# Order of the compressed values' first projection against the keys' GELU in a two-layer decoder trunk

## The chip, the cores and the metric

The kernel runs on one core of a Trainium2 chip. Its time is the device time of one execution in microseconds (us), and the median of several runs is compared. One execution was also taken by the hardware profiler; all rows shown are from it. Engines: PE is TensorE's matmul, PEld its weight load, DVE VectorE, ACT ScalarE, POOL GpSimd, SP SyncE, which here only issues transfers. L714 is line 714 of the kernel.

## The reference

Two layers; each has an input projection into many columns, three token mixers (a convolution, a sparse attention "NSA", a latent attention "MLA"), a cross-attention and a SwiGLU. The change lies in the part of NSA that makes compressed keys and values, and in the projections around it:

```python
z = h @ w_in[layer]                      # 512 tokens, 1024 in
u_glu, q_nsa, kv_nsa, g_nsa, c_q, c_kv, k_rope, g_merge = jnp.split(z, split_at, axis=-1)

def compress_blocks(tok, pos, w1, b1, w2, n_cmp):        # once for keys, once for values
    idx = CMP_STRIDE * arange(n_cmp)[:, None] + arange(CMP_BLOCK)[None, :]   # 31 windows of 32 tokens
    blk = tok[:, idx] + pos[:, None, :]
    blk = ...reshape(bsz, n_cmp, GROUPS, CMP_BLOCK * HEAD_DIM)               # 2048 long
    return gelu(blk @ w1 + b1) @ w2                                          # 2048 -> 256 -> 64

lc = einsum('bqghd,bcgd->bghqc', qb, k_cmp) * scale + bias_c                 # compressed scores
pc = softmax(lc); o_cmp = einsum('bghqc,bcgd->bqghd', pc, v_cmp)
# beside it a selected and a window branch, with the same queries
```

## The kernel before, in words

All matmuls are in float32 made of parts: `unit` and `hilo` split a weight tile or an activation into a high part (ScalarE, L93 to L96) and a remainder (VectorE, L94, L97), and `mm3` (L86 to L88) multiplies three combinations of them. `hTh` and `hTl` hold the normed input so split, `wh` and `wl` (three buffers each) the weights. `fm_blocks` loads two column blocks of 128 (2 x 512 KB) into one of two buffers "raw" and splits them one after the other, each when a `wh` is free. `fm_steps` is one projection: eight steps of three matmuls over 512 tokens, 24 matmuls.

In a layer's `mix` two strands run together. The main strand is the attention: units of scores, softmax and mixture, first the four MLA heads, then the NSA branches. In the MLA part it turns probabilities by TensorE (L865), splits them (PTh by ScalarE, PTl by VectorE L94) and multiplies them with the values one turn later (L878 to L882), with the next head's scores (L843 to L847) between. The other strand is the generator `work`, the filler: `pump(n)` takes n steps of it between the main strand's turns (six in the MLA part). `braid(main, other)` takes two steps of the one and one of the other. So the order of the program is written out by hand, and each engine runs its instructions in an order fixed at compile time, in which what is written first goes first wherever it was expected to be ready. In `work`:

- `projected(windows, i)` projects the tokens of keys (i = 0) or values (i = 1), and `windows` gathers the 31 windows with the position term into `xf` (buffer "gB", four VectorE adds, L649) and splits them into `xt` (L93, L94). The values' `xt` takes the two buffers "BT", used by the keys' weights before and by the bias tables afterwards.
- `compress_in(i)` is the first product, `blk @ w1`: two loads of 1 MB into "raw", eight steps of a split (tile `w`) and four matmuls (L697, L698), into one bank "mm" of PSUM that is held until the GELU. PSUM has three banks "mm".
- `compress_out(i)` has three steps: the GELU (L705 to L710, tile `h`, also in buffer "gB"); its turn by two transposes L714, the split `hT` (L96, L97) and the load of the second weights; and the second product into `kc` or `vc`.
- `projected(stacked_keys, b)` and `projected(stacked_queries, h)` project keys and queries and stack their parts (L409, L410, L416 to L419).
- `conv_steps(m)` projects the two halves of one conv block (16 steps; the bank of the first half, `pa`, is held until both are there), then runs 31 taps on VectorE (L585, L587) at low priority.

`done` and `until` order the strands: the compressed scores (L998, bias added by L1005) ask for "group 0", the product with the compressed values (L1070) for "values". `begin` loads the bias tables (L984) into "BT", and later into "gB". Beside all this, GpSimd's queue issues loads for the SwiGLU of the same layer, one after every few products ("paced").

Of the kernel before, what the change touches and what calls it, by code (L numbers as in the profile page):

```python
# [22 lines left out]
KD = D // 128  # L23
# [10 lines left out]
Z_A, Z_B, Z_Q = 0, 512, 1024  # L34
Z_KC, Z_VC, Z_KS, Z_VS, Z_KW, Z_VW = 1536, 1664, 1792, 1920, 2048, 2176
# [17 lines left out]
def kernel(ctx, tc, x, mem, positions, rel_bias, norm_mix, norm_xattn, norm_mem, norm_ffn, norm_final,  # L53
# [20 lines left out]
    def new(tag, shape=(128, 512), dt=F32, name=None):  # L74
        return (odd if tag in ODD else sb).tile(list(shape), dt, name=name or tag, tag=tag, bufs=BUFS[tag])

    def bank(tag, name=None):
        return ps.tile([128, 512], F32, name=name or f"ps_{tag}", tag=tag, bufs=PBUFS[tag])
# [20 lines left out]
    def load(parts):  # L99
        raw = new("raw", (128, 2048))  # L100
        for view, src in parts(raw):
            nc.sync.dma_start(view, src)
        return raw

    def unit(src, shape):

        n = math.prod(shape)
        h = new("wh", (128, 1024), F32R)
        l = new("wl", (128, 1024), F32R)
        names = " ".join("abc"[:len(shape)])  # L110
        kw = dict(zip("abc", shape))
        hv = h[:, :n].rearrange(f"p ({names}) -> p {names}", **kw) if len(shape) > 1 else h[:, :n]
        lv = l[:, :n].rearrange(f"p ({names}) -> p {names}", **kw) if len(shape) > 1 else l[:, :n]
        hilo(hv, lv, src)
        return hv, lv

    def fm_blocks(w, cols, kt):

        per = 2048 // (kt * 128)
        for i in range(0, len(cols), per):  # L120
            c = cols[i:i + per]
            n = len(c)

            def parts(raw):
                rv = raw[:, :kt * n * 128].rearrange("p (k c) -> p k c", k=kt)
                j = 0
                while j < n:
                    e = j + 1
                    while e < n and c[e] == c[e - 1] + 128:
                        e += 1  # L130
                    yield (rv[:, :, j * 128:e * 128],
                           w[:, c[j]:c[j] + (e - j) * 128].rearrange("(k p) c -> p k c", p=128))
                    j = e
            raw = load(parts)
            rv = raw[:, :kt * n * 128].rearrange("p (k c) -> p k c", k=kt)
            for j in range(n):
                yield unit(rv[:, :, j * 128:(j + 1) * 128], (kt, 128))

    def fm_steps(o, wu, xs, kt, cols=((0, 512),)):
        wh, wl = wu  # L140
        for c0, c1 in cols:
            for k in range(kt):
                yield
                xh, xl = xs(k)
                mm3(o[:, c0:c1], wh[:, k, :], wl[:, k, :], xh[:, c0:c1], xl[:, c0:c1], k == 0, k == kt - 1)
# [325 lines left out]
    def mix(l, x_src, g_mix, x_now, more_x, spill_x, turns):  # L471
        W = w_in[l]
# [98 lines left out]
        def conv_steps(m):  # L571
            for i, wu in enumerate(fm_blocks(W, [Z_A + m * 128, Z_B + m * 128], KD)):
                p = bank("mm")
                yield from fm_steps(p, wu, hx, KD)
                if i == 0:
                    pa = p
            u = new("u", (128, T + TAPS - 1))
            nc.gpsimd.memset(u[:, 0:TAPS - 1], 0.0)
            th = new("ca", name="th")
            nc.scalar.activation(th, p, AF.Tanh, scale=0.5)  # L580
            nc.vector.scalar_tensor_tensor(u[:, TAPS - 1:], th, 1.0, pa, op0=OP.add, op1=OP.mult)
            c = us[m] = new("ca", name="ca")

            tc.cur_priority += 100000
            nc.vector.tensor_scalar(c, u[:, 0:T], cw[:, m, 0:1], cb[:, m:m + 1], op0=OP.mult, op1=OP.add)  # L585
            for j in range(1, TAPS):
                nc.vector.scalar_tensor_tensor(c, u[:, j:j + T], cw[:, m, j:j + 1], c, op0=OP.mult, op1=OP.add)  # L587
            tc.cur_priority -= 100000
# [33 lines left out]
        X = {}  # L622
        K2 = {}
        Q2 = [None] * HEADS
        blocks = fm_blocks(W, [Z_KC, Z_KS, Z_KW, Z_VC] + [Z_Q + 128 * i for i in range(4)], KD)

        def projected(then, *args):
            p = bank("mm")
            yield from fm_steps(p, next(blocks), hx, KD)
            then(p, *args)  # L630
# [42 lines left out]
        def compress_in(i):  # L673
            p = bank("mm")
            b1 = new("vec", (128, 256), name="b1")[0:64]
            vec = (cmp_b1_k, cmp_b1_v)[i]
            nc.scalar.dma_start(b1, bass.AP(tensor=vec.tensor, offset=vec[l].offset, ap=[[0, 64], [1, 256]]))
            hidden[i] = p, b1
            w1 = (cmp_w1_k, cmp_w1_v)[i][l]

            if i == 0:
                w = [t[:, j] for t in (new("BT", (128, 2, 512), F32R, name="w1") for _ in range(2)) for j in range(2)]
            else:
                t = new("o8", (128, 4, 512), F32R, name="w1")
                w = [t[:, j] for j in range(4)]
            w = [v.rearrange("p (k c) -> p k c", k=2) for v in w]
            for k in range(16):
                if k % 8 == 0:
                    raw = load(lambda raw: [(raw.rearrange("p (k c) -> p k c", k=8),
                                             w1[k * 128:(k + 8) * 128, :].rearrange("(k p) c -> p k c", p=128))])  # L690
                    rv = raw.rearrange("p (k c) -> p k c", k=8)
                if k % 2 == 0:
                    wh, wl = w[k % 4:k % 4 + 2]
                    hilo(wh, wl, rv[:, k % 8:k % 8 + 2, :])
                    yield
                x = X[i][k // 8][:, k % 8, :, :]
                nc.tensor.matmul(p[:, 0:256], x, wh[:, k % 2, :], start=k == 0, stop=False)  # L697
                nc.tensor.matmul(p[:, 0:256], x, wl[:, k % 2, :], start=False, stop=k == 15)  # L698
# [44 lines left out]
        done = set()  # L743
# [10 lines left out]
        def braid(main, other):  # L754

            while True:
                for _ in range(2):
                    if next(main, end) is end:
                        return
                    yield  # L760
                if next(other, end) is not end:
                    yield
# [350 lines left out]
        def work():  # L1113

            yield from projected(windows, 0)
            cmp_k, cmp_v = compress_in(0), compress_in(1)
            out_k, out_v = compress_out(0), compress_out(1)
            yield from conv_steps(1)
            yield from braid(projected(stacked_keys, 0), cmp_k)
            yield from braid(projected(stacked_keys, 1), cmp_k)  # L1120
            yield from cmp_k
            yield from projected(windows, 1)
            next(out_k)
            yield from projected(stacked_queries, 0)
            next(out_k)
            yield from braid(projected(stacked_queries, 2), cmp_v)
            next(out_k)
            yield from braid(projected(stacked_queries, 4), cmp_v)
            yield from cmp_v
            next(out_v)  # L1130
            done.add("group 0")
            yield from projected(stacked_queries, 6)
            next(out_v)
            third = conv_steps(2)
            yield from islice(third, 8)
            next(out_v)
            done.update(("values", "group 1"))
            yield from third
            yield from conv_steps(3)

            jobs = {84 + 3 * t: (conv_stats, t) for t in range(NT)} | {99 + 3 * m: (conv_swish, m) for m in range(4)}
            for n, _ in enumerate(chain(merge_steps(2, w_branch_mla[l], o_mla), merge_steps(0, w_branch_conv[l], cS))):
                if n in jobs:
                    yield
                    job, i = jobs[n]
                    job(i)
                yield
# [5 lines left out]
        kv_raw = load(lambda raw: [(raw.rearrange("p (k c) -> p k c", k=2),  # L1153
                                    w_ukv[l].rearrange("(k p) c -> p k c", p=128))])
        filler = work()
        means = bank(next(idle))
        for i, q in enumerate(sq):
# [263 lines left out]
    for l in range(L):  # L1421
# [55 lines left out]
        blocks = fm_blocks(w_xq[l], [128 * h for h in range(4)], KD)  # L1477
# [209 lines left out]
        W = w_gate_up[l]  # L1687
# [150 lines left out]
```

## Time and profile before

| | |
|---|---|
| median of 3 runs | 1897.95 us (1897.93 to 1900.44) |
| the profiled execution | 1898.13 us; span from first to last instruction 1896.4 us |
| granted TensorE clock | 0.999 of full speed |
| busy, share of the span | PE 99%, PEld 87%, DVE 80%, ACT 55%, POOL 14% |
| mixer stage with the change, layer 0 | about 95 to 215 us |
| the same, layer 1 | about 1030 to 1155 us |

A row of the timeline has start, duration, engine, line and operation, written tile and read tiles, the shape, a count, and in brackets how long the engine stood idle before it and for whom. A matmul's duration is modelled and overlaps the next; the distance of two starts is the better measure. A row of a tile has the line, engine and operation, the count, then the shortest, median and longest duration in ns, and the first and last start.

### The profile page before, as it was taken

To read this page: it belongs to the slowest core of one execution; us is meant where nothing else is said; L and a number is where in the kernel's file an instruction comes from. 1 tells how busy PE (TensorE), PEld (TensorE's weight loads), DVE (VectorE), ACT (ScalarE), POOL (GpSimd) and SP (SyncE) were. 2 spreads that over 40 slices of the span, in tenths; PEclk is the share of its full clock that TensorE was granted. 3 is DMA by queue.
4 is the path that set the end of the run, shared out by engine and by line. 5 is a ranking of instruction groups with operands and counts; after the bars stand their busy time and mean duration, and the time that the engine had idled before them with its cause. 6 is when DMAs were issued, how large, how long until landed. Compare 5 with 4: busy or idle time off the path is not lost.

```text
span 1896.4 us, 29494 instructions
## 1 busy us (share of the span) xinstructions
PE 1877.0 (99%) x10988; PEld 1643.5 (87%) x10988; DVE 1509.8 (80%) x2754; ACT 1045.7 (55%) x1952; POOL 269.6 (14%) x433
## 2 busy tenths in 40 slices
PE   9999999999999999999999999999999999999998
PEld 8887888888887999998888878888888879999986
DVE  7999898764466899998869999986645678999886
ACT  5366557763355645456543765676633465454564
POOL 1211111111122211100022111111112221110000
PEclk9999999999999999999999999999999999999999
DMA  6666554455866666656566665435566766766664
GB/s 188 164 155 185 143 129 127 123 147 157 238 180 161 187 163 186 185 181 197 180 181 164 163 197 129 127 100 136 157 182 177 216 165 159 202 164 163 209 191 159
DMA packets 217644, 318.52 MB, mean 168 GB/s; under 512 B 16352, under 2 KB 153843, under 8 KB 217500
## 3 DMA queue, kind: packets, MB, share of 16 engines
q1 hardware_dynamic: 183116, 216.39, 35.9%
q0 software_dynamic: 31872, 94.39, 23.9%
q10 hardware_dynamic: 2512, 5.85, 0.8%
q8 instruction: 86, 1.41, 0.3%
q14 instruction: 58, 0.48, 0.1%
HBM read 307.13 MB, written 97.54 MB: 213 GB/s over the span
## 4 chain that ended last, share of the span: by engine, by line
PE 87%; DVE 5%; issue 4%; ACT 2%; DMA 1%; POOL 1%; POOLq 0%; SPq 0%; DVEq 0%; ACTq 0%
PE ps_mm L86 14%; PE ps_mm L88 14%; PE ps_mm L87 14%; PE ps_s L86 3%; PE ps_s L88 3%; PE ps_s L87 3%; PE ps_t L86 2%; PE ps_t L87 2%; PE ps_t L88 2%; PE ps_t L1083 2%; PE ps_pv L86 1%; PE ps_pv L88 1%; PE ps_pv L87 1%; PE ps_mm L1374 1%; PE ps_mm L1373 1%
## 5 line engine op out<-in xcount | busy, mean ns | idle before, releaser
L93 ACT CAST wh<-raw 128x1024 fp32r<-128x1024 f32 (+3 forms) x419 | 422.8, 1012 | 498.0 <-PE ps_mm L87 123.5
L94 DVE TENSOR_TENSOR wl<-raw,wh 128x1024 fp32r<-128x1024 f32 (+3 forms) x419 | 488.6, 1172 | 221.6 <-ACT wh L93 218.4
L86 PE MATMUL ps_mm<-hTh,wh 128*128 128x512 f32 (+1 forms) x1152 | 414.6, 360 | 0.5 <-DVE kc L94 0.5
L87 PE MATMUL ps_mm<-hTl,wh 128*128 128x512 f32 (+1 forms) x1152 | 411.2, 357 | 0.0
L88 PE MATMUL ps_mm<-hTh,wl 128*128 128x512 f32 (+1 forms) x1152 | 410.5, 357 | 0.5 <-DVE wl L94 0.5
L88 PEld LDWEIGHTS ps_mm<-hTh,wl 128*128 128x128 f32 x1152 | 217.8, 189 | 32.7 <-DVE wl L94 1.3
L86 PEld LDWEIGHTS ps_mm<-hTh,wh 128*128 128x128 f32 x1152 | 217.9, 189 | 29.4 <-issue 1.3
L87 PEld LDWEIGHTS ps_mm<-hTl,wh 128*128 128x128 f32 x1152 | 217.9, 189 | 26.3 <-issue 0.7
L587 DVE SCALAR_TENSOR_TENSOR ca<-u,vT,ca 128x512 f32<-128x512 f32 x240 | 177.5, 747 | 2.9
L466 POOL DMA_DIRECT2D up<-in_w_gate_up_dram x128 | 85.0, 664 | 538.6 <-PE ps_mm L88 380.9
L466 POOL DMA_DIRECT2D down<-in_w_down_dram x132 | 85.3, 646 | 478.6 <-PE ps_mm L88 255.2
L93 ACT CAST PTh<-ps_t 128x512 fp32r<-128x512 f32 (+4 forms) x136 | 70.6, 519 | 53.2 <-PE ps_t L1083 39.6
L1046 ACT ACTIVATE P<-P,ss 128x512 f32<-128x512 f32 (+3 forms) x128 | 71.6, 560 | 49.2 <-DVE ss L1043 48.2
L86 PE MATMUL ps_s<-rh,wh 128*128 128x256 f32 x320 | 90.6, 283 | 0.0
L87 PE MATMUL ps_s<-rl,wh 128*128 128x256 f32 x320 | 90.6, 283 | 0.0
L88 PE MATMUL ps_s<-rh,wl 128*128 128x256 f32 x320 | 90.6, 283 | 0.0
L94 DVE TENSOR_TENSOR PTl<-ps_t,PTh 128x512 fp32r<-128x512 f32 (+2 forms) x120 | 71.6, 598 | 9.0 <-ACT PTh L93 7.9
L1054 ACT ACTIVATE P<-P,sr 128x512 f32<-128x512 f32 (+3 forms) x128 | 63.3, 555 | 16.9 <-DVE sr L1052 16.8
L86 PE MATMUL ps_mm<-op,wh 128*128 128x512 f32 (+1 forms) x192 | 68.8, 359 | 0.0
L88 PE MATMUL ps_mm<-op,wl 128*128 128x512 f32 (+1 forms) x192 | 68.4, 356 | 0.3
L87 PE MATMUL ps_mm<-op,wh 128*128 128x512 f32 (+1 forms) x192 | 68.0, 355 | 0.0
L86 PEld LDWEIGHTS ps_s<-rh,wh 128*128 128x128 f32 x320 | 61.4, 192 | 0.0
(567 smaller groups left out, 4652.0 us busy)
## 6 DMA issues: line engine op xcount, KB each, us to landing
up<-in_w_gate_up_dram POOLq DMA_DIRECT2D x128, 320.0 KB, 4.4
down<-in_w_down_dram POOLq DMA_DIRECT2D x132, 256.0 KB, 4.3
raw<-in_w_in_dram SPq DMA_DIRECT2D x32, 1024.0 KB
raw<-in_w_gate_up_dram SPq DMA_DIRECT2D x60, 512.0 KB
raw<-up SPq DMA_DIRECT2D x40, 512.0 KB
raw<-down SPq DMA_DIRECT2D x40, 512.0 KB
raw<-in_w_down_dram SPq DMA_DIRECT2D x30, 512.0 KB
raw<-in_w_in_dram SPq DMA_DIRECT2D x26, 512.0 KB
```

Source lines behind the costliest of these rows:

```text
L86: nc.tensor.matmul(o, lh, rh, start=start, stop=False)
L87: nc.tensor.matmul(o, lh, rl, start=False, stop=False)
L88: tick(nc.tensor.matmul(o, ll, rh, start=False, stop=stop))
L93: nc.scalar.copy(hi, src)
L94: nc.vector.tensor_tensor(lo, src, f(hi), op=OP.subtract)
L466: d = nc.gpsimd.dma_start(dst, src, accum_op=op) if op else nc.gpsimd.dma_start(dst, src)
L587: nc.vector.scalar_tensor_tensor(c, u[:, j:j + T], cw[:, m, j:j + 1], c, op0=OP.mult, op1=OP.add)
L1046: nc.scalar.activation(p[:, c], p[:, c], AF.Exp, bias=s[:, k:k + 1], scale=-1.0, accum_out=s[:, 4 + k:5 + k])
L1054: nc.scalar.activation(P[k], P[k], AF.Copy, scale=r[:, k:k + 1])
L1083: nc.tensor.transpose(tp[:, w:w + 128], P[k][:, j * 128:(j + 1) * 128], ident)
L1373: nc.tensor.matmul(accs[t], xh, u[0][:, k, :], start=j == 0, stop=False)
L1374: nc.tensor.matmul(accs[t], xh, u[1][:, k, :], start=False, stop=False)
```

## The change

The load pairs change, because blocks must come in the order of use: keys, selected keys, window keys, queries 0, values, queries 1, 2, 3 (each block of queries is two heads). In `work` the values' projection with its windows moves behind the step that turns the keys' GELU (second step of `compress_out(0)`). The values' first product is no longer braided with queries 1 and 2 but with queries 2 and with the first half of the third conv block (eight steps), which was behind queries 3 before. "group 0" is marked after queries 1.

```diff
-        blocks = fm_blocks(W, [Z_KC, Z_KS, Z_KW, Z_VC] + [Z_Q + 128 * i for i in range(4)], KD)
+        blocks = fm_blocks(W, [Z_KC, Z_KS, Z_KW, Z_Q, Z_VC] + [Z_Q + 128 * i for i in range(1, 4)], KD)
...
             yield from cmp_k
-            yield from projected(windows, 1)
             next(out_k)
             yield from projected(stacked_queries, 0)
             next(out_k)
-            yield from braid(projected(stacked_queries, 2), cmp_v)
+            yield from projected(windows, 1)
             next(out_k)
+            yield from projected(stacked_queries, 2)
+            done.add("group 0")
             yield from braid(projected(stacked_queries, 4), cmp_v)
+            third = conv_steps(2)
+            yield from braid(islice(third, 8), cmp_v)
             yield from cmp_v
             next(out_v)
-            done.add("group 0")
             yield from projected(stacked_queries, 6)
             next(out_v)
-            third = conv_steps(2)
             yield from islice(third, 8)
             next(out_v)
             done.update(("values", "group 1"))
             yield from third
```

## The prediction

> **What bounds the kernel now.** First the core's span with the granted clock, and the page's line of busy times: TensorE decides.
>
> ```profile
> core 0: 1896.4 us, clock 0.999
> ```
>
> ```profile
> PE 1877.0 (99%) x10988; PEld 1643.5 (87%) x10988; DVE 1509.8 (80%) x2754; ACT 1045.7 (55%) x1952; POOL 269.6 (14%) x433
> ```
>
> The change neither adds nor removes a matmul, so it can only act on the gaps between them. Second, then, the list of TensorE's waits, cut to the stretch of each layer where the change lies (first layer 0, then layer 1; columns: what waited, for whom, us in total, times, longest).
>
> ```profile
> PE ps_pv L881 <- DVE PTl L94: 1.2, 1, 1.2
> PE ps_mm L714 <- DVE h L710: 0.4, 1, 0.4
> PE ps_t L86 <- DVE op L410: 0.4, 1, 0.4
> PE ps_mm L698 <- DVE w L94: 0.3, 1, 0.3
> PE ps_mm L86 <- DVE kc L94: 0.3, 1, 0.3
> PE ps_pv L880 <- ACT PTh L93: 0.2, 1, 0.2
> ```
>
> ```profile
> PE ps_pv L881 <- DVE PTl L94: 1.2, 1, 1.2
> PE ps_mm L88 <- DVE wl L94: 0.5, 1, 0.5
> PE ps_mm L714 <- DVE h L710: 0.4, 1, 0.4
> PE ps_mm L86 <- DVE kc L94: 0.3, 1, 0.3
> PE ps_pv L880 <- ACT PTh L93: 0.2, 1, 0.2
> ```
>
> Both layers show the same cluster: L880, L881 and L714 wait one after the other, mostly for VectorE. Third, the timeline of TensorE gives its full price, since a stream that stopped also restarts slowly. The first two rows show the undisturbed distance of matmuls of 512 columns. From L847 on come L847, L880, L881 and L882, four of that width, and the two transposes L714, in layer 0 and then in layer 1.
>
> ```profile
> 158.04 0.39 PE L846 MATMUL ps_s<-op 128*128 128x512 f32 x1
> 158.26 0.39 PE L847 MATMUL ps_s<-op 128*128 128x512 f32 x1
> ...
> 161.69 0.33 PE L714 MATMUL ps_mm<-ident,h 62*128 62x62 f32 x2 [0.44 <-DVE h L710]
> 161.96 0.50 PE L86 MATMUL ps_mm<-hTh,wh 128*128 128x512 f32 x1
> ```
>
> ```profile
> 1096.72 0.39 PE L847 MATMUL ps_s<-op 128*128 128x512 f32 x1
> ...
> 1100.37 0.51 PE L86 MATMUL ps_mm<-hTh,wh 128*128 128x512 f32 x1
> ```
>
> The two rows are 0.22 apart; the times are rounded, and over longer runs it is 0.23. Undisturbed, then, this takes 4 x 0.23 and 0.27 for L714 (161.96 less 161.69), 1.19 us. It takes 3.70 and 3.65, so 2.51 and 2.46 us are lost, 4.97 us in all. Against the listed waits of a layer (1.2, 0.4 and 0.2, 1.8 us) that is a factor of 1.4, which I use for other waits below.
>
> Fourth, why VectorE is late: the 10 us that hold the cluster's main wait (columns: us, then busy us and count of PE, PEld, DVE, ACT, POOL, and the granted clock), and the rows of the tiles h (the GELU) and xf (the values' windows), with first and last start in layer 0.
>
> ```profile
> 151.00:161.00 10.00, 8.63 (x48) 6.87 (x46) 9.78 (x21) 6.90 (x16) 0.95 (x2) 1.00 0.49 133
> ```
>
> ```profile
> L714 PE MATMUL ps_mm<-ident,h x4: 221/246/270, 161.7 to 190.2; 62*128 62x62 f32 x4
> L705 DVE TENSOR_TENSOR h<-ps_mm,b x2: 410/414/417, 155.7 to 181.9; 62x256 f32<-62x256 f32 x2
> ...
> L710 DVE SCALAR_TENSOR_TENSOR h<-h x2: 406/412/418, 161.2 to 186.5; 62x256 f32<-62x256 f32 x2
> ```
>
> ```profile
> L649 DVE TENSOR_TENSOR xf<-ps_mm,vT x8: 659/672/677, 96.7 to 153.5; 64x496 f32<-64x496 f32 x8
> ```
>
> ```profile
> L94 DVE TENSOR_TENSOR xt<-xf,xt x8: 402/410/419, 99.5 to 155.0; 128x248 fp32r<-128x248 f32 x8
> ```
>
> In the code xf and the GELU's h1 share the one buffer "gB". The trace agrees: L705 starts at 155.7, when the last split xt that reads xf (155.0, 0.41 long) is over. So the keys' GELU stands behind the whole burst of the values' windows (4 x 0.67 and 4 x 0.41, 4.3 us of VectorE), and the softmax's split PTl stands between its five steps.
>
> **The change part by part.**
>
> **The order.** Now the turn of the GELU (L714) comes ahead of the values' projection. By then h1 has only the keys' old xf ahead of it, gone since about 100 us; the keys' product ends one projection and one turn of the attention ahead of the burst, whose four L649 end at 154.2: 154.2 less 4 x 0.67, 24 x 0.23 and some 1.5 is about 144 (an estimate), so L705 can start there and not at 155.7. Between it and L714 lies one projection, 24 matmuls of 0.23 us and a turn of the attention, as now lies between L705 of the values (181.9) and its L714 (190.2); of the two turns in layer 0 only one is in the list of waits, and the values' isn't. So I take the cluster's 4.97 us as gone. Bounds: 4.97 gone to nothing gone.
>
> **The burst by itself.** It stays, some 10 us after the GELU's start instead of ahead of it, and can make the next split late. The nearest rows are the keys' windows, which start at 96.7: their neighbourhood has the wait for op L410 (0.4) in layer 0 and for wl L94 (0.5) in layer 1, 0.9 us, times 1.4 makes 1.26 us. Bounds: 0, because none of the listed waits of layer 0 falls between 144 and 158, while the burst ran, and 4.97, the whole cluster again.
>
> **PSUM banks.** "mm" has three. Now the compressed keys' product holds one while the values' hidden sum holds another, hence the wait for kc: 0.3 in each layer, times 1.4 and twice 0.84 us, which goes, since the hidden sum begins only after it. In its place conv's first half (pa) is held over the last queries and the turn of the values' GELU. The second half must then wait for a bank from the turn (hT, read last by L97) or from the queries (op L410):
>
> ```profile
> L97 DVE SCALAR_TENSOR_TENSOR hT<-ps_mm,hT x1: 254/254/254, 193.9 to 193.9; 128x124 fp32r<-128x124 f32 x1
> ```
>
> ```profile
> L998 PE MATMUL ps_s<-kc,op x4: 276/277/277, 188.0 to 188.4; 128*128 128x64 f32 x4
> ```
>
> ```profile
> 189.26 0.40 PE L86 MATMUL ps_mm<-hTh,wh 128*128 128x512 f32 x1
> ```
>
> L97 ends at 194.15, 3.85 us after L714 (190.3); one turn of the attention (from the scores L998 to the next projection's matmul) covers 1.25 (189.26 less 188.0). So the bounds are 0 and 2.6 us a layer. The same kind of shortage cost 0.42 (kc). I take a quarter of the way from 0.42 to 2.6, 0.97, as the kc row is the only one that is such a wait: +1.93 us in both layers.
>
> **Loads.** The pairs of one load are now [keys' window, queries 0] and [values, queries 1]; the queries 0 and 1 were one transfer and become halves of two others, one more issue on SP's queue a layer (0.4 us, idle otherwise). The first projection's second half of weights is asked for when the first half is split, as now; its wait (w L94, 0.3) I leave. The load of conv's pair moves ahead of it on SP. ScalarE's load of b1 and GpSimd's four small memsets of xt move with their steps; both have 5 us and more until their readers, and behind the memsets in GpSimd's queue stand only the paced loads for the later down- and up-projection. Cost nothing, unless the third rival holds.
>
> **Values ready later.** vc comes one half of conv later: 24 x 0.23 and 1.25, 6.8 us.
>
> ```profile
> L738 DVE CAST vc<-vc x1: 282/282/282, 197.7 to 197.7; 32x256 fp32r<-32x256 f32 x1
> L1070 PEld LDWEIGHTS ps_pv<-PTh,vc x1: 187/187/187, 217.4 to 217.4; 128*128 128x128 f32 x1
> ```
>
> Its reader comes 19 us after it, so this costs nothing; without that cover it would be 6.8 us.
>
> **The bias table.** Its second half takes the buffer of the values' windows, free when the first projection ends. In the program that end moves from step 89 of the filler to step 97, and the compressed scores L998 are written after step 96; so in time it moves from 181.9 to about 188.0. (The mark "group 0", which they ask for, falls at step 73 and not 89: reached either way, so its own move costs and gains nothing.)
>
> ```profile
> L1005 DVE TENSOR_TENSOR Pc<-ps_s,BT x4: 223/235/253, 189.9 to 235.0; 128x62 f32<-128x62 f32 x2, 128x46 f32<-128x46 f32 x2
> L984 SPq DMA_DIRECT2D BT<-vd x2: 366/368/371, 172.0 to 181.9; - x2
> ```
>
> ```profile
> 195.33 0.43 DVE L94 TENSOR_TENSOR PTl<-ps_t,PTh 128x256 fp32r<-128x256 f32 x1
> ```
>
> ```profile
> 307.11 4.59 DMA BT<-vd
> ```
>
> ```profile
> 200.47 0.28 PE L881 MATMUL ps_pv<-PTl,op 128*128 128x256 f32 x1
> ```
>
> Asked for at 188.0 and 0.37 plus 4.59 us on its way, it lands near 193.0, and the second L1005 would run at 190.1: VectorE would stand still for 2.9 us, with all behind it. Its next split PTl (195.8 at its end) is read at 200.5, 4.7 us later, so 0 on TensorE; without that cover 2.9 us a layer. The Trainium skill's page "DMA: Bandwidth & Descriptors" (Anatomy of one DMA) gives 2.0 us plus bytes over 436 GB/s for GpSimd's queue, an estimate of 3.2 us for these 512 KB: by it VectorE would stand for 1.5 us. The trace's 4.59 for the same table decides.
>
> **Sum.** -4.97 - 0.84 + 1.26 + 1.93 = -2.62 us. The profiled execution took 1898.13 (span 1896.4 and 1.7 around it), 0.2 above the median of 1897.95; so 1895.5 against it and 1895.3 for the median.
>
> **The rivals.** *All waits go:* neither burst nor bank costs anything; -5.81, 1892.1 us. For it: no wait while the burst ran; against it: three banks are few, and VectorE is busy for 9.8 of 10 us here.
>
> *The wait only moves:* VectorE's work is the same and its queue full, so the late split comes back at the burst's new place, as large; 1897.9. For it that busy share; against it that the values' GELU, after an equal projection, made nobody wait.
>
> *The weights' load comes too late (slower):* there are two "raw" buffers, and between the two halves of the first projection's weights now stands conv's load, while [queries 2, queries 3] still holds the other. If queries 3 is split only after conv's first weights, the second half waits for two loads in a row.
>
> ```profile
> 167.95 5.84 DMA raw<-in_cmp_w_v_dram
> ```
>
> ```profile
> 144.65 0.39 ACT L93 CAST wh<-raw 128x256 fp32r<-128x256 f32 x1
> ```
>
> Two loads of 5.84 and five splits of about 1 to 1.2 come to some 17 us; cover are the 6.6 us until its first use (174.5, by the order of now) and the last queries' 24 x 0.23; about 5.4 us are left a layer, 1906. It decides from 3.2 us a layer, where it outweighs the rest by over 0.2%. Against it: weights are split well ahead of their turn where a buffer is free (the keys' second projection was split at 144.65 and used at 169). The Trainium skill's page "TensorE: Matmul & The Clock Gate" (Part 1) has TensorE fall to half its clock after an idle window of about 3.4 us; by that each such gap would cost up to 1.7 us more, 1909. No wait here is longer than 1.2 us and the granted clock is 0.999 over the span, so no row tests it.
>
> *The table stops VectorE beyond its cover:* +2.9 a layer, 1901.
>
> **How the numbers follow.** The forecast 0.48, all waits go 0.20, it only moves 0.17, the load 0.10, the table 0.05. Within 0.2% (3.8 us, about what a measurement of this kernel can tell from no change) lies the forecast but for a third of it; faster 0.20 + 0.16 = 0.36; slower the load, most of the table and a little of the third, 0.16; the same 0.48. The likeliest case alone reaches from 1893 to 1898. The range, 1891.0 to 1900.0, leaves out the load, half the table and the best of the first rival.
>
> **What would show it.** L705 of the keys starts by 147, and L714 and L881 near it wait for nobody: then the order works. A PTl wait after the later L649 refutes the burst's price; ps_mm L86 waiting for hT or op L410 near conv's second half shows the bank's. L1005 idle for BT shows the table. Loads of w_in: two of 1 MB fewer, four of 512 KB more. Wrong I would be above all if waits of over 1 us for raw or for a bank appear.

## The result, and the profile after

The changed kernel takes 1909.88 us (median of 6 runs, 1907.88 to 1912.69), the kernel before 1898.60 (6 runs beside them): a ratio of 1.0056, 95% interval 1.0046 to 1.0067, so 11.3 us slower. The forecast was 1895.3 with a range up to 1900.0; what came is in the main the third rival, "the weights' load comes too late", which stood at 1906, and 1909 with the clock's rule. The profiled execution is the longest of the six; its span and busy times:

```profile
core 0: 1911.0 us, clock 0.995
PE 1884.1 (99%) x10988; PEld 1648.4 (86%) x10988; DVE 1511.2 (79%) x2754; ACT 1044.3 (55%) x1952; POOL 269.0 (14%) x433
```

The work is the same; the span is 14.6 us longer and the clock 0.004 lower. TensorE's waits in the two stretches in which the change lies (layer 0, then layer 1; columns as before the change):

```profile
PE ps_mm L86 <- ACT wh L93: 2.5, 1, 2.5
PE ps_s L1038 <- DVE Pc L1006: 1.2, 1, 1.2
PE ps_pv L880 <- ACT PTh L93: 0.7, 1, 0.7
PE ps_t L86 <- DVE op L410: 0.4, 1, 0.4
```

```profile
PE ps_mm L86 <- ACT wh L93: 3.0, 1, 3.0
PE ps_mm L86 <- DVE vc L94: 2.6, 1, 2.6
PE ps_pv L880 <- ACT PTh L93: 0.7, 1, 0.7
PE ps_mm L88 <- DVE wl L94: 0.5, 1, 0.5
```

The rows for PTl, for h and for kc are gone: what the change aimed at it did. In their place stand waits that are longer than any of before; the new order also makes TensorE wait for conv's weights (wh). The lists add up to 11.6 us against 5.4 before. Most of the rest is the clock. Windows around the waits (columns: us, busy us and count of PE, PEld, DVE, ACT and POOL, the granted clock, DMA share, GB/s):

```profile
180.00:183.40 3.40, 3.27 (x10) 2.79 (x11) 3.08 (x6) 2.82 (x7) 0.46 (x2) 0.50 0.42 158
204.00:207.40 3.40, 3.40 (x10) 2.65 (x9) 2.52 (x9) 2.12 (x5) 0.36 (x1) 0.51 1.11 373
1125.00:1129.00 4.00, 3.68 (x11) 3.10 (x12) 3.55 (x7) 3.46 (x8) 0.95 (x2) 0.57 0.38 142
1153.00:1160.00 7.00, 4.43 (x13) 3.34 (x12) 5.26 (x13) 3.85 (x6) 1.07 (x3) 0.76 0.55 143
```

Four times TensorE runs at half its clock for some 3.4 us, 1.7 us lost each time (4.00 x 0.43, 7.00 x 0.24), 6.8 us in all; the kernel before has no such stretch until its last matmuls are done. So 6.2 us of waits and 6.8 of clock, 13.0 of the 14.6, are accounted for. This holds for the profiled execution; the six runs differ in clock, 0.994 to 0.998, so the clock's share is not the same in each.

Why conv's weights are late is read from three queues: SyncE's issues, ScalarE's splits and TensorE, all in layer 0.

```profile
152.74 0.37 SPq L102 DMA_DIRECT2D raw<-in_cmp_w_v_dram  x1
175.47 0.99 SPq L102 DMA_DIRECT2D raw<-in_w_in_dram  x2
184.74 10.83 SPq L102 DMA_DIRECT2D raw<-in_cmp_w_v_dram  x2
```

```profile
173.97 0.60 ACT L93 CAST w<-raw 128x512 fp32r<-128x512 f32 x1
179.03 1.04 ACT L93 CAST wh<-raw 128x1024 fp32r<-128x1024 f32 x1 [0.64 <-DMA raw<-in_w_in_dram]
182.41 1.05 ACT L93 CAST wh<-raw 128x1024 fp32r<-128x1024 f32 x1
```

```profile
177.26 0.39 PE L880 MATMUL ps_pv<-PTh,op 128*128 128x384 f32 x1
180.13 0.80 PE L86 MATMUL ps_mm<-hTh,wh 128*128 128x512 f32 x1 [2.48 <-ACT wh L93]
```

One raw buffer holds the first half of the values' weights until its last split (173.97); the other holds [queries 2, queries 3] until queries 3 is split, which in the order of the code comes behind conv's first weights: ScalarE's row at 179.03 is conv's, the one at 182.41 is queries 3's. So conv's pair can be asked for only at 175.47 and lands 3.55 us later (ScalarE's split at 179.03 waits for it), and the weights' second half can be asked for only at 184.74. Before the change that half was asked for at 167.95. The first matmul of conv stops TensorE for 2.5 us here and 3.0 in layer 1.

### The profile page after: what moved, and what is told of

The parts are those of the page before. It is cut to its first block, busy times and chain, and to the rows that moved or that the text cites. A ratio compares the mean times of both kernels' runs of the same rounds, so it can differ in the third digit from the quotient of the medians.

```text
span 1911.0 us, 29496 instructions
## 1 busy us (share of the span) xinstructions
PE 1884.1 (99%) x10988; PEld 1648.4 (86%) x10988; DVE 1511.2 (79%) x2754; ACT 1044.3 (55%) x1952; POOL 269.0 (14%) x433
## 4 chain that ended last, share of the span: by engine, by line
PE 84%; DVE 6%; issue 4%; DMA 3%; ACT 2%; POOL 1%; SPq 0%; POOLq 0%; DVEq 0%; ACTq 0%
PE ps_mm L86 14%; PE ps_mm L88 14%; PE ps_mm L87 13%; PE ps_s L86 3%; PE ps_s L88 3%; PE ps_s L87 2%; PE ps_t L86 2%; PE ps_t L87 2%; PE ps_t L88 2%; PE ps_t L1083 2%; PE ps_pv L86 1%; PE ps_pv L88 1%; PE ps_pv L87 1%; PE ps_mm L1375 1%; PE ps_mm L1376 1%
## 5 line engine op out<-in xcount | busy, mean ns | idle before, releaser
L86 PE MATMUL ps_mm<-hTh,wh 128*128 128x512 f32 (+1 forms) x1152 | 417.4, 363 | 8.2 <-ACT wh L93 5.5
L86 PEld LDWEIGHTS ps_mm<-hTh,wh 128*128 128x128 f32 x1152 | 218.9, 190 | 39.1 <-ACT wh L93 6.6
L86 PE MATMUL ps_s<-rh,wh 128*128 128x256 f32 x320 | 90.6, 283 | 0.0
L86 PE MATMUL ps_mm<-op,wh 128*128 128x512 f32 (+1 forms) x192 | 68.8, 359 | 0.0
L86 PEld LDWEIGHTS ps_s<-rh,wh 128*128 128x128 f32 x320 | 61.4, 192 | 0.0
```

Of the source, the lines that this page charges most:

```text
L86: nc.tensor.matmul(o, lh, rh, start=start, stop=False)
```

## The experiments

Theory A: the two raw buffers are the bound; conv's load between the halves of the values' weights makes two loads come one after the other. Its rivals: the new order costs by itself, through VectorE's queue or the three "mm" banks. All ratios below are to runs of the kernel before beside them (its median there 1899.09, 1899.56, 1899.39, 1899.13 and 1900.43 us for 1 to 4, 5 to 8, 9 and 10, 11, and 12). Where an edit adds lines, the numbers of later lines grow by one to three: L699 of experiment 1 is L697 of the changed kernel. "..." marks code left out.

**1. Queries 3 split ahead of conv's weights.**

```
+            ahead.append(next(blocks))          # queries 3's weights
             third = conv_steps(2)
             yield from braid(islice(third, 8), cmp_v)
...
-            yield from fm_steps(p, next(blocks), hx, KD)
+            yield from fm_steps(p, ahead.pop(0) if ahead else next(blocks), hx, KD)
```

> The changed order, with one thing added: queries 3 take their split weights (high and low part) ahead of the third conv block, not after it; loads, pairs and all matmuls are the same. Theory A (the loss comes from a held 'raw' buffer: buffers 'wh' are handed out in written order, so queries 3 cannot be split before conv's first block, whose load waits for the very buffer that queries 3 hold): conv's pair is asked for by about 162 in layer 0 instead of 175.5, the second half of the first projection's weights by 176 instead of 184.7, the wait of ps_mm L86 for wh (2.5 and 3.0 us) goes, the granted clock is back at 0.999, and the time is 1892 to 1898 us. Theory B (braiding the product with conv is itself the loss, by the banks 'mm' and VectorE): at least half of the 11 us stays, 1904 or more.

Measured: 1901.45 us, ratio 1.0008 (0.9999 to 1.0017), between the two ranges. One early split takes the loss from 11.3 us to 2.4. SyncE's issues, and TensorE's wait in layer 0:

```profile
167.49 1.00 SPq L102 DMA_DIRECT2D raw<-in_w_in_dram  x2
175.45 0.37 SPq L102 DMA_DIRECT2D raw<-in_cmp_w_v_dram  x1
```

```profile
PE ps_mm L699 <- ACT w L93: 2.6, 1, 2.6
```

Conv's pair now comes 8 us earlier and nobody waits for it, but the second half of the weights is next in line for a buffer and 2.6 us late (2.5 in layer 1), with half clock after each. Theory A holds for the main loss; its expectation that nothing would be late behind it does not.

**2. Without conv between the halves.** The move and the pairs of loads stay; conv's first half comes after the values' product, as before the change.

```
-            third = conv_steps(2)
-            yield from braid(islice(third, 8), cmp_v)
+            yield from braid(projected(stacked_queries, 6), cmp_v)
             yield from cmp_v
             next(out_v)
-            yield from projected(stacked_queries, 6)
+            third = conv_steps(2)
+            yield from islice(third, 8)
```

> The values' projection stays behind the turn of the keys' GELU, but the first product is braided with queries 2 and queries 3, and conv's first half comes after it, between the GELU of the values and its turn. Theory A: no third load stands between the two halves of the weights, so nothing is late: 1891 to 1896 us, faster than before by the cluster of 5 us or most of it. Theory B: the same, since conv is out of the braid. Theory C (the move of the values' windows itself costs, because VectorE's burst only changes place): 1897 or more.

Measured: 1897.56 us, ratio 0.9991 (0.9982 to 0.9999): the loss is gone with the braid of conv. The time is in theory C's range, not in A's, but no wait stands at the windows' burst, as C had it. The gain of the move is nearly used up by a new wait, the values' GELU at its turn (layer 0, layer 1); ScalarE stands for a load beside it:

```profile
PE ps_mm L714 <- DVE h L710: 2.3, 1, 2.3
PE ps_mm L714 <- DVE h L710: 1.6, 1, 1.6
```

```profile
190.25 0.30 ACT L93 CAST wh<-raw 128x128 fp32r<-128x128 f32 x1 [3.27 <-DMA raw<-in_cmp_w_v_dram]
```

**3. The move alone, the product braided a step earlier** (queries 2 and queries 4, right behind the windows).

```
-            yield from projected(stacked_queries, 2)
-            done.add("group 0")
+            yield from braid(projected(stacked_queries, 2), cmp_v)
             yield from braid(projected(stacked_queries, 4), cmp_v)
-            third = conv_steps(2)
-            yield from braid(islice(third, 8), cmp_v)
...
+            third = conv_steps(2)
             yield from islice(third, 8)
```

> Only the move of the values' projection with the load pairs that it needs; the first product is braided with queries 1 and 2 as before, which is now right behind the windows' burst. Theory A: the loads are as before, so no late weights; the cluster (5 us) is gone, but the product needs the values' windows 2 us after their projection, while the burst takes over 4 us on VectorE: some 0 to 2 us come back in each layer; 1893 to 1898 us. Theory C: 1898 or more, with waits for PTl or xt after the burst.

Measured: 1900.47 us, ratio 1.0005 (0.9996 to 1.0014): no difference from before, and what theory C foresaw, a wait for xt behind the burst. Layer 0 (in layer 1 the two waits are 2.0 and 1.9 us):

```profile
PE ps_mm L697 <- DVE xt L94: 1.7, 1, 1.7
PE ps_mm L697 <- ACT w L93: 1.1, 1, 1.1
```

Here the product stands directly behind the windows and waits for their splits; in the changed kernel queries 2 lies between, and no xt row appears.

**4. The braid alone.** The windows and the pairs of loads as before the change, the braid with queries 4 and conv's first half as in the changed kernel.

```
-        blocks = ... [Z_KC, Z_KS, Z_KW, Z_Q, Z_VC] + [Z_Q + 128 * i for i in range(1, 4)] ...
+        blocks = ... [Z_KC, Z_KS, Z_KW, Z_VC] + [Z_Q + 128 * i for i in range(4)] ...
...
+            yield from projected(windows, 1)
             next(out_k)
             yield from projected(stacked_queries, 0)
             next(out_k)
-            yield from projected(windows, 1)
-            next(out_k)
             yield from projected(stacked_queries, 2)
+            next(out_k)
```

> The other half of the change alone: the values' windows at their old place and the old load pairs, but the first product braided with queries 2 and with conv's first half. Theory A: [queries 2, queries 3] holds a 'raw' buffer in the same way, so conv's pair and the second half of the weights are asked for as late as in the changed kernel; the keys' cluster stays as well: 1906 to 1915 us. Theory C (the move is what costs): near 1898 us.

Measured: 1911.24 us, ratio 1.0063 (1.0051 to 1.0076).

```profile
176.57 1.17 SPq L102 DMA_DIRECT2D raw<-in_w_in_dram  x2
...
186.26 10.05 SPq L102 DMA_DIRECT2D raw<-in_cmp_w_v_dram  x2
```

```profile
PE ps_mm L86 <- ACT wh L93: 1.3, 1, 1.3
PE ps_mm L714 <- DVE h L710: 1.6, 1, 1.6
```

The same two late issues, without the move, and a time in theory A's range. But the late weights do not appear as one long wait here: wh takes 1.3 us in layer 0 (rows above) and 0.7 in layer 1, and the rest is spread over other rows, L714 (1.6 in each layer, 0.4 before), PTh (1.7 in each) and vc (1.5) above all; 13.3 us are listed against 5.4 before. With 2 this settles which part of the change costs: the braid of conv, some 12 us. That most of it comes from the two buffers is shown for the changed kernel by 1, and not separately here. The move gains 1.5 us in 2 and nothing in 3, where the product stands right behind the windows.

Left open were why the cluster's 4.97 us were not gained even there, and why the values' GELU is late.

**5. The values' second weights in a buffer of their own** (on 2).

```
-            raw = load(lambda raw: ...)
+            raw = new("u", (128, T + TAPS - 1), name="w2") if i else new("raw", (128, 2048))
+            for c in range(0, n, 64):
+                nc.sync.dma_start(...)
```

> The variant without the braid of conv's first half (queries 0 with the values in one load, the move of the windows kept) lost 2.3 and 1.6 us at the values' L714 and then 1.7 us at half clock. Here the small load of the values' second weights (64 KB) goes to a buffer of the conv's shifted inputs instead of one of the two raw buffers; nothing else differs. Theory A (whatever asks for a raw buffer late lands late: ScalarE stood 3.27 us for these weights, and behind them in its queue stood the split of the queries that VectorE's GELU waited behind): L714 waits for nobody, 2.3 + 1.6 + 1.7 = 5.6 us less than the 1897.6 of that variant, 1892.0 (1890.5 to 1894). Rival (the values' GELU has simply too few steps until its turn): L714 still waits 1.5 to 2.5 us in each layer, 1896 to 1898.

Measured: 1901.99 us, ratio 1.0013 (1.0005 to 1.0022), slower than either range. ScalarE's stand is gone and the wait is longer (2.9 and 2.5 us, half clock after both). VectorE in layer 0:

```profile
194.17 0.25 DVE L1006 TENSOR_TENSOR Pc<-ps_s,BT 128x62 f32<-128x62 f32 x1 [3.02 <-DMA BT<-vd]
```

Three of the GELU's five steps on VectorE were done by 190.5; the fourth stands behind this step of the compressed softmax, which waits for the second half of the bias table. Theory A's reading of 2 was wrong: the small load was not what decided.

**6. The kernel before, with the GELU's h apart from the windows' xf** (the order of steps untouched).

```
-            both = new("gB", (128, 2, 512), name="h1")
-            h1, u = (both[0:64, c, 0:256] for c in range(2))
+            both = new("u", (128, T + TAPS - 1), name="h1")
+            h1, u = (both[0:64, c:c + 256] for c in (0, 256))
```

> The kernel before, in its old order of steps; only the GELU's h and u lie in a buffer of the conv's shifted inputs instead of sharing gB with the windows' xf. Theory A of the first step (the shared buffer, not the written order, put the keys' GELU behind the values' windows): the first L705 starts before 150 instead of at 155.7, and the cluster L880, L881, L714 loses nothing: 4.97 us less than the kernel before, 1894 (1892.5 to 1896). Rival (the order of steps does it, or the burst of the windows makes the splits late by itself): the waits at 158 to 162 stay and the time is within 2 us of the kernel before.

Measured: 1898.92 us, ratio 0.9995 (0.9986 to 1.0004): no difference, the rival's time. The tile h, then TensorE's waits of layer 0:

```profile
L705 DVE TENSOR_TENSOR h<-ps_mm,b x4: 397/410/419, 143.6 to 1122.4; 62x256 f32<-62x256 f32 x4
```

```profile
PE ps_mm L698 <- DVE w L94: 1.3, 1, 1.3
PE ps_mm L697 <- ACT w L93: 1.0, 1, 1.0
PE ps_mm L86 <- DVE kc L94: 0.9, 1, 0.9
```

The shared buffer was indeed what held the GELU (143.6 instead of 155.7, and no row for L714, L880 or L881), yet 3.2 us of other waits come in its place, 2.4 in layer 1 (kc 0.9, w 0.8 and 0.7). TensorE now comes to the third pair of w some 1.8 us sooner (L697 at 166.04; before at 167.88), but the weights are no sooner there: ScalarE stands for a load of w_in, and VectorE's split of w behind it starts at 166.85 instead of 165.48.

```profile
163.76 1.05 ACT L93 CAST wh<-raw 128x1024 fp32r<-128x1024 f32 x1 [1.51 <-DMA raw<-in_w_in_dram]
```

The later splits free the raw buffer later, so the second half is asked for at 169.49 instead of 167.95. The bank of kc is free only 0.4 us sooner.

**7. The changed kernel with 1, with conv's first steps by themselves, the second half braided with the last queries, the values' product behind the next conv block's first half, and 5's buffer.**

```
-            yield from braid(islice(third, 8), cmp_v)
+            yield from islice(third, 8)
+            yield from braid(projected(stacked_queries, 6), cmp_v)
             yield from cmp_v
-            next(out_v)
-            yield from projected(stacked_queries, 6)
             next(out_v)
             yield from islice(third, 8)
             next(out_v)
+            yield from third
+            fourth = conv_steps(3)
+            yield from islice(fourth, 8)
+            next(out_v)
...
```

> The changed kernel with queries 3 split ahead of conv's weights, conv's first eight steps written by themselves, and the second half of the values' first projection braided with the last queries (so that half's weights have eight more steps to land); the values' second weights lie apart as in the variant before the last. Theory A (the rest of the loss with queries 3 early, 2.6 and 2.5 us at L699 and 1.7 us at half clock twice, was the second half's weights): L699 waits under 0.5 us, and the 1901.5 of that variant falls by some 8 us to 1893 (1891.5 to 1896). Rival B (the order of steps itself overloads VectorE or the three mm banks): other waits of 1 to 3 us come in their place, 1898 to 1903.

Measured: 1901.58 us, ratio 1.0007 (0.9998 to 1.0016).

```profile
PE ps_mm L86 <- DVE op L410: 2.3, 1, 2.3
PE ps_s L1041 <- DVE Pc L1009: 1.1, 1, 1.1
```

L699 waits no more, but a matmul waits for a bank that the last queries leave late (2.2 in layer 1). Here the rival is right.

**8. Sixteen steps between the values' GELU and its turn** (on 2).

```
             next(out_v)
-            third = conv_steps(2)
-            yield from islice(third, 8)
+            yield from conv_steps(2)
             next(out_v)
-            yield from islice(third, 8)
+            fourth = conv_steps(3)
+            yield from islice(fourth, 8)
             next(out_v)
...
```

> The variant without the braid of conv's first half, with sixteen steps of conv instead of eight between the values' GELU and its turn L714, and the values' product eight steps later still; the loads as they were. Theory A: the 3.3 us that ScalarE stands for the values' second weights remain, but eight more steps (24 matmuls of 0.23 us) cover them: L714 waits for nobody, 1892 (1890.5 to 1895). Rival (whoever comes behind ScalarE's wait is late all the same): the wait goes over to conv's weights wh or to a bank at L86, 1 to 3 us a layer, 1896 to 1900.

Measured: 1899.07 us, ratio 0.9996 (0.9987 to 1.0005).

```profile
PE ps_mm L698 <- DVE w L94: 1.5, 2, 1.3
PE ps_mm L86 <- ACT th L580: 1.1, 1, 1.1
```

L714 is free, and two others wait, as the rival said.

**9. The table's second half, and the GELU's h, in other buffers** (on 5).

```
-  tab = new("gB" if g == 1 and r == 0 else "BT", (128, 2, 512))
+  tab = new("gB" if g == 0 and r == 1 else "BT", (128, 2, 512))
```

The GELU's h moves as in 6.

> The variant with the values' second weights apart waited 2.9 and 2.5 us at the values' L714, because VectorE stood 3.0 us for the second half of the bias table (it takes the buffer of the values' windows, free only when their projection ends) with the GELU behind it, and 3.4 us went at half clock. Here that half of the table takes the windows' sum's old buffer gB, and the GELU's h lies with the conv's shifted inputs; the order of steps is unchanged. Theory A (the table is the wait): VectorE waits for no BT near 190, L714 waits under 0.5 us in each layer, no half clock: 2.9 + 2.5 + 3.4 = 8.8 us less than that variant's 1902.0, 1893 (1891 to 1896). Rival (the compressed softmax's own steps, now earlier, still stand ahead of the GELU, or the 1024-wide splits do): L714 waits 1 to 2.5 us still, 1896 to 1901.

Measured: 1898.59 us, ratio 0.9998 (0.9990 to 1.0007), outside theory A's range. L714 waits no more and VectorE has no row for BT, so the table was the wait of 5; but in its place L86 waits for wh, 1.2 and 0.9 us, and half clock follows once. That is the rival's time by another mechanism than the rival's. The profiled execution took 1901.53 us, so its half clock need not be in the runs near the median.

**10. Both: 9's buffers and 8's steps.**

> The same buffers as in the variant with the table apart, and sixteen steps of conv instead of eight between the values' GELU and its turn. Theory A: with both the load and the table off the GELU's way and twice the cover, L714 waits for nobody; the waits that the sixteen-step variant showed (1.3 us at L698 for split weights, 1.1 to 1.4 us at L86 for a bank that conv's tanh holds) come from the order and stay in part: 1893 to 1897. Rival (a wait only moves on, since VectorE is busy for over 9 of 10 us from 125 to 185): the time stays at the 1899.1 of the sixteen-step variant, within 1.5 us.

Measured: 1897.41 us, ratio 0.9992 (0.9983 to 1.0001), 1.7 us below 8, between the two ranges. In both layers one wait of size is left, in layer 0:

```profile
PE ps_mm L698 <- DVE w L94: 1.6, 2, 1.3
```

In VectorE's queue two 1024-wide splits of later weights (1.22 us each) stand ahead of these of 0.69.

**11. On 10: the splits of the values' first weights go first on ScalarE and VectorE.**

```
-  hilo(wh, wl, rv[:, k % 8:k % 8 + 2, :])
+  tc.cur_priority -= 1000 * i; hilo(wh, wl, rv[:, k % 8:k % 8 + 2, :]); tc.cur_priority += 1000 * i
```

> The variant with sixteen steps and all buffers apart; only the splits of the values' first weights are given priority over the other work ready on ScalarE and VectorE (there the 1024-wide splits of conv's weights stood ahead of them, and L698 waited 1.3 us in each layer, 1.5 with what follows). Theory A (that wait is VectorE's order and nothing else is behind it): L698 waits under 0.4 us, 1897.4 less 2 x 1.5 is 1894.4 (1893 to 1896). Rival (VectorE has no room: the split that is put back makes another matmul wait): a wait of 1 us or more in each layer on wl, xt, kc or op in its place, 1896.5 to 1899.

Measured: 1894.66 us (1893.88 to 1895.57), ratio 0.9975 (0.9966 to 0.9985). The time is that of theory A, and this version beats both kernels, by 4.5 us the kernel before. All that TensorE waits for in layer 0's stretch:

```profile
PE ps_mm L88 <- DVE wl L94: 0.5, 1, 0.5
PE ps_mm L698 <- DVE w L94: 0.4, 1, 0.4
PE ps_t L86 <- DVE op L410: 0.4, 1, 0.4
```

**12. The same buffers and priority in the old order of steps.**

> The kernel before, in its own order of steps and loads, with what the best variant has besides the order: the GELU's h, the values' second weights and the table's second half each in a buffer apart, and the splits of the values' first weights ahead. Theory A (the buffers and the split's place in the queues carry the gain; the order only decides what collides): the cluster at 158 to 162 is gone and L697, L698 wait under 0.5 us; the bank wait for kc (0.9) stays: 1895 to 1896.5. Rival (the moved order is needed too, because in the old one the second half of the weights is asked for too late): L697 waits 1 us or more for w in each layer, 1897.5 to 1899.5.

Measured: 1905.96 us (1902.11 to 1907.76), ratio 1.0033 (1.0021 to 1.0046), outside both. Layer 0, layer 1:

```profile
PE ps_mm L86 <- DVE kc L94: 1.6, 1, 1.6
PE ps_mm L86 <- DVE kc L94: 2.3, 1, 2.3
```

The bank that the compressed keys' product holds while the hidden sum of the values holds another, 0.3 us before, is the wait now. So the buffers and the priority alone do not carry the gain: the new order, in which no row for kc appears, is needed too. The profiled execution is the shortest of its runs (1902.11); what lengthens the others by up to 5.7 us no profile shows, and stays open.

## Why the prediction was wrong, point by point

**The order: mechanism right, its worth not.** L705 was put at about 144 and came at 143.2; L714 follows at 149.28 with no wait.

```profile
L705 DVE TENSOR_TENSOR h<-ps_mm,b x4: 395/407/417, 143.2 to 1141.2; 62x256 f32<-62x256 f32 x4
```

```profile
149.28 0.30 PE L714 MATMUL ps_mm<-ident,h 62*128 62x62 f32 x2
```

The 4.97 us left the cluster. But experiment 6 shows that they were also cover of what comes next: with only the cluster gone, 5.6 us of listed waits for w and kc stand there, where there had been 0.9. The prediction asked what would be late next for the burst, the bank and the table, and for the loads only in a rival.

**The burst: 1.26 predicted, 0 found.** Between 110 and 176 us the changed kernel's list of TensorE's waits is empty. Experiment 3 shows its price without cover: 1.7 us at L697, and 2.0 in layer 1.

**The bank: the wait that was priced did not come, another did.** 0.97 us a layer was taken for conv's second half, waiting for the turn's hT or the queries' op. That half waits for nobody. In layer 1, and not in layer 0, the first matmul of the next conv block waits for the bank of the compressed values' product:

```profile
1156.12 0.71 PE L86 MATMUL ps_mm<-hTh,wh 128*128 128x512 f32 x1 [2.56 <-DVE vc L94]
```

The product is done by 1152.6, but its split on ScalarE starts only at 1155.52, behind steps of the softmax. That the wait is as long as the prediction's upper bound (2.6) is chance, since the bound was worked out for hT. Half clock follows, which the term had no place for.

**The loads: the step that failed.** It read "Cost nothing, unless the third rival holds", and the third rival held. The argument against it, that weights are split well ahead where a buffer is free, came from a row of a time when a buffer was free; here none was. The rival's cause was right (queries 3 holds the buffer behind conv's first weights); its place was half right, since the load first missed is conv's own pair (wh, 2.5 and 3.0), while the second half, asked for 16.8 us later than before, lands behind attention's work. Its price of 5.4 us a layer (17 less 6.6 and 5.5 would be 4.9) compares with 2.5 and 3.0 of waits and 1.7 of clock for each, 4.2 and 4.7. That is 8.9 us in all that the prediction had at nothing, and it is the larger part of the 14.6. In experiment 1 both waits are gone, and the loss falls from 11.3 us to 2.4, though others change with them (vc and Pc go, L699 comes). The rival had a chance of 0.10; the code's written order of splits and the count of two buffers, both in the prediction's own text, would have borne far more.

**The clock.** The prediction gave the rule of the Trainium skill, "TensorE: Matmul & The Clock Gate" (Part 1), only as a figure beside the rival, 1909. The trace agrees with the rule's price, 3.4 us at half clock, 1.7 lost, but not with its trigger of an idle window of about 3.4 us: 2.5 us were enough. The same page of the Trainium skill also calls that window free-running, which fits the mixed outcomes of shorter waits (last section).

**Values later: cost right, delay not.** vc comes 13 us later in layer 0 (210.8 instead of 197.4), where 6.8 were foreseen; its first reader, at 223.9, waits for nobody.

**The table: the stop was seen, its cover was not whole.** VectorE stood for it, less long than the 2.9 us foreseen, since the GELU came later too; but its next split PTl was not the first thing to suffer. A scores matmul of the attention waits for the bank that the table's step reads:

```profile
200.73 0.26 DVE L1005 TENSOR_TENSOR Pc<-ps_s,BT 128x62 f32<-128x62 f32 x1 [1.43 <-DMA BT<-vd]
```

```profile
202.37 0.51 PE L1038 MATMUL ps_s<-op 128*128 128x512 f32 x1 [1.23 <-DVE Pc L1006]
```

Between the two rows VectorE also runs a split of 1.22 us. In experiment 1, with the same buffers, the table is asked for at 190.10 instead of 195.92, VectorE stands 0.25 us for it and no scores matmul waits: the table was late because the weights were. In experiment 5 the stop grew to 3.02 us and put 2.9 on L714. The fourth rival's mechanism was thus a small part of the loss, 1.2 us in layer 0 only and a share in the half clock behind it.

## What to carry to other kernels

Before a step is put between two loads, count the staging buffers and write down, for each load, which split must have run before it can be asked for; the written order of the splits sets that. A wait on the critical engine is cover for whatever comes next: taking it away pays only as far as the next transfer, bank and split are early too, and here it took five edits besides the new order to gain 4.5 us, about what one cluster of waits seemed to be worth; which of the five could be left out was not tested. When a stall of TensorE grows past some 2 us (here 2.2 to 3.0), add what the clock does after it.

## What the runs showed of the hardware that was not expected

Half clock after short waits. In the profiled executions of the changed kernel and of the twelve experiments, every single listed wait of 2.2 to 3.0 us in the stretches looked at (11 of them) is followed by a stretch at a granted clock of 0.50. In ten cases it lasts about 3.4 us, in one, after 2.5 us in experiment 5's layer 1, about twice as long:

```profile
1136.00:1138.00 2.00, 2.00 (x6) 1.52 (x6) 0.94 (x3) 1.27 (x3) 0.00 (x0) 0.50 0.97 328
1138.00:1140.00 2.00, 2.00 (x7) 1.52 (x6) 0.66 (x1) 0.00 (x0) 0.00 (x0) 0.50 0.11 40
```

Single waits of 1.0 to 2.0 us are not followed by one (1.6 at L714 in experiment 2, layer 1; 2.0 at L697 in experiment 3, layer 1). Two waits close together are mixed: 0.70 and 1.23 us within 2 us led to the stretch at 204 quoted above, and so did 1.2 and 0.5 in experiment 9, 1.1 and 0.3 in experiment 3's layer 0, and 1.0 and 0.5 in experiment 4's layer 1; but 1.9 and 0.3 in experiment 3's layer 1 led to none. The kernel before, whose longest wait there is 1.2 us, has none.

The runs of the changed kernel differ in time as in clock: 1907.88 us at 0.998 and 1912.69 at 0.995, 4.8 us, about three such stretches. Profiled executions at 0.997 and 0.998 had one or two of them (experiments 1 to 4, 7 and 9). So the same program does not have all four in every run; whether the waits are shorter there, or not followed by half clock, no profile shows.
